# A decoder step on one core: an earlier verdict, later first squares, a second pass without GpSimd, a branch hint, paired last multiplications and stores on two queues

## The chip, the core and the metric

The kernel runs on one core of a Trainium2 chip. The time is device microseconds of one launch. The kernel before took 1876.56 us (median of three runs, 1875.29 to 1877.31).

## The reference

One layer of a hybrid decoder over 264 tokens (256 of a new sequence, 8 single tokens that continue old ones), model width 2048, feed-forward width 5504:

```
h = h + 0.5 * swiglu(rmsnorm(h, norm_ffn1), ffn1_gate, ffn1_up, ffn1_down)
h = h + mixing_block(rmsnorm(h, norm_mix), ...)     # mLSTM heads and a short gated convolution
h = h + 0.5 * swiglu(rmsnorm(h, norm_ffn2), ffn2_gate, ffn2_up, ffn2_down)
y = rmsnorm(h, norm_final)
rmsnorm(x, g) = x * rsqrt(mean(x*x) + EPS) * g
swiglu(x, wg, wu, wd) = (silu(x @ wg) * (x @ wu)) @ wd
```

All inputs and weights are 32-bit floats. The new states of the mixing block are outputs too.

## The kernel before

**Layout.** The width lies on the 128 partitions in KB = 16 blocks, the T = 264 tokens in the free dimension. `h` is 16 tiles of 128x264, two by two in the `hpair` tiles.

**Products.** Each 32-bit weight is split in two 16-bit parts, `whi` (ACT, `high`, L178) and `wlo` (DVE, `low`, L186); each activation likewise, `x[:, 0]` and `x[:, 1]`. `three` (L223) issues three matmuls for one 128x128 block of weights: hi by hi (L224), hi by lo (L225), lo by hi (L226). `fetch` (L192) loads one piece of weights of up to 512 KB through the SP queue and splits it; six buffers each of `wraw`, `whi` and `wlo` let it run ahead. `product` (L228) makes one 128x264 result out of 16 blocks (48 matmuls) and calls `fetch` between its halves.

**The order.** There is no scheduler (`manual_schedule`): each engine runs what the program issues, in that order. `at(n, f)` puts `f` off to a later `tick`; each `product` ticks once at its start and by a half within it.

**The start.** `products4` (L249) makes the first four results (gate and up of two blocks) at once, in nine groups: per group one or two blocks of `h` are loaded, cut in two parts (`Norm.cut`) and squared (`Norm.square`, L372: every second block on ACT, the others on GpSimd, and GpSimd adds them up in `acc`), and a piece of weights serves 24 matmuls (12 in the first two groups). `Norm.finish` (L384) sums `acc` over the partitions with a matmul by ones (`column_sums`, L349) and takes the reciprocal root. It stands right behind `products4` on TensorE.

**The end.** After each of the last 16 products `done` (L459) squares the block on GpSimd and multiplies it by its gain. Behind the last one the root is taken (L329 on ACT, L335 to L341 on DVE), DVE multiplies the 16 blocks by it (L480), and SP stores them (L482, L484).

**The verdict.** 16-bit parts can overflow or lose too much. So `watch` (L288) puts a sum of magnitudes of each result into `stat`, `watch_norm` (L299) two values of each norm's sums into `squares`, and `judge` (L308) tests them against bounds. After the multiplications, the last `judge` calls and matmuls by ones make `bad`, 0 or 1. All five engines load it (L109) and branch on it (L110): if it is 1, the whole step is done again in 32-bit parts, which is a copy of the program of about the same length that stands between the branch and the end. In the usual case all engines jump over it. GpSimd has, behind the jump, an instruction (INC_SWDGE_SEM) that raises the semaphores of its DMA queue as if the copy had run.

Of the kernel before, what the change touches and what calls it, by code (L numbers as in the profile page):

```python
# [8 lines left out]
F32 = mybir.dt.float32  # L9
# [7 lines left out]
SEQ = 256  # L17
# [21 lines left out]
NSTAT = 320  # L39
FIRST = [(0, 1), (1, 1)] + [(k, 2) for k in range(2, KB, 2)]  # L40
# [62 lines left out]
def hymba_step(tc: tile.TileContext, a: dict):  # L103


    with tc.tile_pool(name="verdict", bufs=1) as pool:
        bad = pool.tile([1, 1], mybir.dt.int32, name="bad")
        step(tc, a, bad)
        again = tc.nc.values_load(bad, min_val=0, max_val=1)  # L109
    with tc.If(again > 0):  # L110
        step(tc, a)
# [3 lines left out]
def step(ctx: ExitStack, tc: tile.TileContext, a: dict, bad=None):  # L115
    nc = tc.nc
    PSUM = bass.MemoryType.PSUM
# [4 lines left out]
    AHEAD = 5 if half_size else 2  # L122

# [16 lines left out]
    nc.gpsimd.dma_start(bg, a["bg"])  # L140
# [25 lines left out]
    ident = const.tile([128, 128], F32, name="ident")  # L166
    make_identity(nc, ident)
# [115 lines left out]
    if half_size:  # L283
        stat = const.tile([128, NSTAT], F32, name="stat")
        nc.gpsimd.memset(stat, 2.0 * SUMS[0])
        squares = const.tile([128, 8], F32, name="squares")
# [69 lines left out]
    class Norm:  # L356
# [5 lines left out]
        def block(self, kb, by_act=False):  # L362
            self.cut(kb)
            self.square(kb, by_act)
# [7 lines left out]
        def square(self, kb, by_act=False):  # L372
            new = self.acc is None
            sq = t264("acc", 1) if new else t264("sq")
            if by_act:
                nc.scalar.activation(sq, h[kb], AF.Square)  # L376
            else:
                nc.gpsimd.tensor_tensor(sq, h[kb], h[kb], op=ALU.mult)  # L378
            if new:
                self.acc = sq  # L380
            else:
                nc.gpsimd.tensor_tensor(self.acc, self.acc, sq, op=ALU.add)  # L382

        def finish(self, *rest, last=False):  # L384

            self.r = t264("rstd", 1)
            self.ssum = column_sums(self.acc, *rest)
# [5 lines left out]
    def ffn(layer, norm, done, start=None):  # L393
        with tc.tile_pool(name=f"act_{norm.tag}", bufs=1) as apool:
            first = True
            for half, blocks in enumerate(HALVES):
                act = {}
                for i, j in enumerate(blocks):
                    if start is not None and j < 2:
                        if j == 0:  # L400
                            ps4 = start()
                        pg, pu = ps4[2 * j : 2 * j + 2]
                    else:
                        pg = product((layer, "g", j), norm.x, range(KB))
                        pu = None
# [8 lines left out]
                    if pu is None:  # L414
                        pu = product((layer, "u", j), norm.x, range(KB))
# [19 lines left out]
    def ahead(part):  # L435
# [5 lines left out]
        for kb in range(k0, k0 + n):  # L441
            n1.block(kb, kb % 2 == 0)
# [9 lines left out]
        bank=bank, at=at, tick=tick, watch=watch, high=high, low=low, PART=PART, s3=s3,  # L452
# [6 lines left out]
    def done(kb):  # L459
# [12 lines left out]
    def judge_early():  # L472
        early.append(len(stats))
        judge(stat[:, : early[0]], SUMS)

# [3 lines left out]
    for kb in range(KB):  # L479
        nc.vector.tensor_tensor(h[kb], h[kb], nf.r, op=ALU.mult)  # L480
        if kb < 2:
            nc.sync.dma_start(a["yt"][:, kb, :], h[kb])  # L482
        elif kb % 2:
            nc.sync.dma_start(a["yt"][:, kb - 1 : kb + 1, :], hpair[kb // 2])  # L484

    if half_size:
        watch_norm(nf.ssum)
        judge(stat[:, early[0] : len(stats)], SUMS)
        judge(squares, SQUARES)
        ps = bank()[:1, :1]  # L490
        for i, v in enumerate(verdicts):
            nc.tensor.matmul(
# [593 lines left out]
```

## Time and profile before

| | us |
|---|---|
| three runs, median (range) | 1876.56 (1875.29 to 1877.31) |
| the profiled execution | 1874.37 |
| its span, first to last instruction | 1872.5 |
| time outside the span | 1.87 |
| `products4` on TensorE, first to last matmul | 6.34 to 34.1 |
| last matmul of the last product ends | 1846.9 |
| `bad` is written | 1858.59 |
| last instruction | 1872.5 |

The span counts to the last instruction on any engine, the waiting of sequencers at the end included. Rows of the sequencers (names with a q: SPq, POOLq) are branches, semaphore waits, drains and DMA issues; they are not counted as busy. A time line gives the start and the duration in us, then engine, line, instruction and tiles, and in brackets how long the engine had been idle and what released it.

### The profile page before, as it was taken

Reading aid. Unit: us, or ns where it says so; the run is one execution under the profiler, and the core shown is the slowest. Engines: PE = TensorE matmul, PEld = TensorE weight load, DVE = VectorE, ACT = ScalarE, POOL = GpSimd, SP = SyncE. Lnnn points to the kernel's source line nnn. Section 1 sums busy time; section 2 is a strip of 40 time slices with the busy share of each in tenths; the row PEclk is TensorE's granted clock in tenths of the full one; section 3 lists DMA queues with packets and bytes.
Section 4 is the critical chain, followed back from the end, with each engine's and each line's share of the span. In section 5 each row is a group of like instructions: output and inputs, shape, how many; then the busy total and the mean of one; then the engine's idle time right before and its main releaser. Section 6 shows DMA issues by size and latency. Waiting matters only on the chain.

```text
span 1872.5 us, 38560 instructions
## 1 busy us (share of the span) xinstructions
PE 1830.6 (98%) x16107; PEld 1586.8 (85%) x16107; DVE 1191.9 (64%) x1910; ACT 859.6 (46%) x1211; POOL 146.8 (8%) x219
## 2 busy tenths in 40 slices
PE   8999999999999999999999899999999999999994
PEld 6888888888888888888888688888888888888884
DVE  8666655466666557888888666666655456666453
ACT  6444443344444444656566645444443434444441
POOL 5000000000000211211211021000000000000110
PEclk9999999999999999999999999999999999999997
DMA  7666565656565555878778565656656656655551
GB/s 263 215 198 200 185 206 187 207 189 198 190 199 181 201 187 189 280 236 290 263 236 296 167 206 188 207 188 196 202 189 192 206 187 197 202 188 186 197 192 54
DMA packets 114714, 381.11 MB, mean 204 GB/s; under 512 B 14797, under 2 KB 19997, under 8 KB 114529
## 3 DMA queue, kind: packets, MB, share of 16 engines
q1 hardware_dynamic: 106048, 350.79, 57.4%
q0 software_dynamic: 8192, 27.57, 4.3%
q8 instruction: 128, 2.10, 0.4%
q14 instruction: 58, 0.47, 0.1%
q10 hardware_dynamic: 288, 0.19, 0.1%
HBM read 366.72 MB, written 11.78 MB: 202 GB/s over the span
## 4 chain that ended last, share of the span: by engine, by line
PE 82%; DVE 9%; issue 3%; ACT 2%; DMA 2%; POOL 0%; SPq 0%; DVEq 0%; ACTq 0%; POOLq 0%
PE ps L225 27%; PE ps L224 27%; PE ps L226 27%; DVE wlo L186 3%; DMA rb<-dr 1%; DVE cs L842 1%; ACT whi L178 1%; DVE jk L853 1%; ACT jk L861 1%; ACT L329 0%; DMA wraw<-in_w1gu 0%; DVE x L186 0%; DVE qkv L514 0%; DVE h L480 0%; DVE rs_q L338 0%
## 5 line engine op out<-in xcount | busy, mean ns | idle before, releaser
L186 DVE SCALAR_TENSOR_TENSOR wlo<-wraw,whi 128x1024 f16<-128x1024 f32 (+2 forms) x683 | 787.7, 1194 | 233.7 <-ACT whi L178 233.5
L226 PE MATMUL ps<-x,wlo 128*128 128x264 f16 x2752 | 759.6, 276 | 4.3 <-DVE wlo L186 4.3
L224 PE MATMUL ps<-x,whi 128*128 128x264 f16 x2752 | 759.6, 276 | 1.6 <-ACT whi L178 1.4
L225 PE MATMUL ps<-x,whi 128*128 128x264 f16 x2752 | 759.6, 276 | 0.0
L178 ACT ACTIVATE whi<-wraw 128x1024 f16<-128x1024 f32 (+2 forms) x683 | 664.9, 1016 | 165.5 <-PE ps L225 159.3
L226 PEld LDWEIGHTS <-wlo 128*128 128x128 f16 (+1 forms) x5296 | 518.6, 98 | 84.4 <-DVE wlo L186 6.5
L225 PEld LDWEIGHTS <-whi 128*128 128x128 f16 (+1 forms) x5296 | 518.6, 98 | 81.2 <-issue 1.8
L224 PEld LDWEIGHTS <-whi 128*128 128x128 f16 (+1 forms) x5296 | 518.6, 98 | 80.2 <-ACT whi L178 2.1
L224 PE MATMUL ps<-a,whi 128*128 128x264 f16 x1376 | 379.8, 276 | 0.0
L225 PE MATMUL ps<-a,whi 128*128 128x264 f16 x1376 | 379.8, 276 | 0.0
L226 PE MATMUL ps<-a,wlo 128*128 128x264 f16 x1376 | 379.8, 276 | 0.0
L224 PE MATMUL ps<-xm,whi 128*128 128x264 f16 (+1 forms) x912 | 252.3, 277 | 0.0
L225 PE MATMUL ps<-xm,whi 128*128 128x264 f16 (+1 forms) x912 | 252.3, 277 | 0.0
L226 PE MATMUL ps<-xm,wlo 128*128 128x264 f16 (+1 forms) x912 | 252.2, 276 | 0.0
L178 ACT ACTIVATE a<-tc 128x264 f16<-128x264 f32 x86 | 36.4, 423 | 295.0 <-DVE tc L418 292.6
L413 ACT ACTIVATE tb<-ta 128x264 f32<-128x264 f32 x86 | 36.3, 423 | 224.0 <-DVE ta L410 222.1
L425 DVE SCALAR_TENSOR_TENSOR h<-ps,h 128x264 f32<-128x264 f32 x64 | 27.7, 433 | 159.5 <-PE ps L226 159.5
L417 DVE TENSOR_TENSOR tc<-ps,rstd 128x264 f32<-128x264 f32 x86 | 37.1, 432 | 94.5 <-PE ps L226 94.5
L378 POOL TENSOR_TENSOR acc<-h 128x264 f32<-128x264 f32 x3 | 1.9, 626 | 1177.0 <-DVE stat L294 589.1
L410 DVE TENSOR_TENSOR ta<-ps,rstd 128x264 f32<-128x264 f32 x86 | 37.2, 432 | 60.4 <-PE ps L226 60.2
L186 DVE SCALAR_TENSOR_TENSOR a<-tc,a 128x264 f16<-128x264 f32 x86 | 37.3, 433 | 42.2 <-ACT a L178 42.2
L382 POOL TENSOR_TENSOR acc<-acc,sq 128x264 f32<-128x264 f32 x59 | 55.2, 936 | 6.4 <-ACT sq L376 1.8
(184 smaller groups left out, 864.8 us busy)
## 6 DMA issues: line engine op xcount, KB each, us to landing
wraw<-in_w2gu SPq DMA_DIRECT2D x172, 512.0 KB, 4.9
wraw<-in_w1gu SPq DMA_DIRECT2D x171, 512.0 KB, 4.8
wraw<-in_win SPq DMA_DIRECT2D x112, 512.0 KB, 5.5
wraw<-in_w1d SPq DMA_DIRECT2D x80, 448.0 KB, 4.1
wraw<-in_w2d SPq DMA_DIRECT2D x80, 448.0 KB, 4.0
wraw<-in_wout SPq DMA_DIRECT2D x32, 512.0 KB, 4.5
rb<-dr POOLq DMA_DIRECT2D x16, 513.0 KB, 10.2
wraw<-in_w1d SPq DMA_DIRECT2D x16, 512.0 KB, 4.4
```

Source lines behind the costliest of these rows:

```text
L178: nc.scalar.activation(dst, src, AF.Copy, scale=scale)
L186: nc.vector.scalar_tensor_tensor(dst, src, scale, hi, op0=ALU.mult, op1=ALU.subtract)
L224: nc.tensor.matmul(ps, wh, xk[:, 0, :], start=first, stop=False)
L225: nc.tensor.matmul(ps, wh, xk[:, 1, :], start=False, stop=False)
L226: nc.tensor.matmul(ps, wl, xk[:, 0, :], start=False, stop=last)
L382: nc.gpsimd.tensor_tensor(self.acc, self.acc, sq, op=ALU.add)
L410: nc.vector.tensor_tensor(zg, pg, norm.r, op=ALU.mult)
L413: nc.scalar.activation(sg, zg, AF.Silu)
L417: nc.vector.tensor_tensor(zu, pu, norm.r, op=ALU.mult)
L425: nc.vector.scalar_tensor_tensor(h[db], ps, 0.5 / (sw * sa[layer]), h[db], op0=ALU.mult, op1=ALU.add)
L842: nc.vector.scalar_tensor_tensor(c[:, b, eb], rb[:, b, HD : 2 * HD], self.v[eb][:, col : col + 1], c[:, b, eb], op0=ALU.mult, op1=ALU.add,)
L853: nc.vector.tensor_tensor(jk, c, rb[:, :, :HD].unsqueeze(2).to_broadcast([128, 2, 2, HD]), op=ALU.mult)
```

## The change

**Start.** The first block of `h` is loaded through SP ahead of the first weights, the vectors through ACT alone. `products4` only cuts the blocks. The squares are taken on ACT by pairs of blocks (128x528) behind it, at ticks 0, 1, 1.5 and 2, and GpSimd adds seven pairs into the first. Two products more (gate and up of the third block) come ahead of `norm.finish`, whose sum is made of two matmuls, one for each half of the pair. So the four first results wait in their banks for two products.

**End.** The 16 multiplications become eight of 128x528, and the stores, one for each, go to SP and ACT in turn. The sums of the last norm are tested by an added ACT instruction (L508) that writes into `stat`. The tests of the other norms move to the early `judge`, eight products ahead of the end; the last test is two DVE instructions, of which the second counts, and one more matmul. It stands behind the first multiplication, and `bad` is written behind the second.

**The branch.** Only SP, ACT, TensorE and DVE load `bad` and branch. The second pass uses SP's queue and DVE where the first uses GpSimd (`queue`, `side`), so that no GpSimd instruction is left in it, and takes its mask from `beyond`, which the first pass makes. A bounds check of the loaded value is left out. A hint, "likely taken", stands ahead of the branch on the four engines, behind `bad`.

```diff
+BRANCHING = [getattr(mybir.EngineType, e) for e in ("SP", "Activation", "PE", "DVE")]
...
-    with tc.tile_pool(name="verdict", bufs=1) as pool:
-        step(tc, a, bad)
-        again = tc.nc.values_load(bad, min_val=0, max_val=1)
-    with tc.If(again > 0):
-        step(tc, a)
+        step(tc, a, shared, bad)
+        again = nc.values_load(
+            bad, engines=BRANCHING, min_val=0, max_val=1,
+            skip_runtime_bounds_check_because="a comparison writes 0 or 1",
+        )
+        with tc.If(again > 0, label="again"):
+            step(tc, a, shared)
...
+    queue = nc.gpsimd if half_size else nc.sync
+    side = nc.gpsimd if half_size else nc.vector
...
-    nc.scalar.dma_start(h[0], a["xt"][:, 0, :])
     nc.scalar.dma_start(vecs, a["vecs"])
+    nc.sync.dma_start(h[0], a["xt"][:, 0, :])
...
+        def square_pairs(self, pool, pairs):
+            for i in pairs:
+                tag = f"sq{min(i, 1)}"
+                sq = pool.tile([128, 2, T], F32, tag=tag, name=tag, bufs=1 + 2 * min(i, 1))
+                nc.scalar.activation(sq, hpair[i], AF.Square)
+                if i == 0:
+                    self.acc = sq
+                else:
+                    side.tensor_tensor(self.acc, self.acc, sq, op=ALU.add)
...
+                    if first and start is not None:
+                        ps4 = start()
+                        for n, ps in enumerate(ps4):
+                            early[n // 2, "gu"[n % 2]] = ps
+                        for step, pairs in ((0, (0, 1)), (1, (2, 3)), (1.5, (4, 5)), (2, (6, 7))):
+                            at(step, norm.square_pairs, apool, pairs)
+                        tick(0)
+                        for which in "gu":
+                            early[2, which] = product((layer, which, 2), norm.x, range(KB))
...
-            n1.block(kb, kb % 2 == 0)
+            n1.cut(kb)
...
+                nc.scalar.activation(
+                    t264("ta"), nf.ssum, AF.Copy, scale=2.0**10, accum_out=stat[:, j : j + 1]
+                )
...
+    def scaled(i):
+        r = nf.r.unsqueeze(1).to_broadcast([128, 2, T])
+        nc.vector.tensor_tensor(hpair[i], hpair[i], r, op=ALU.mult)
+        queues[i % 2].dma_start(a["yt"][:, 2 * i : 2 * i + 2, :], hpair[i])
+
+    scaled(0)
     if half_size:
-        watch_norm(nf.ssum)
-        judge(stat[:, early[0] : len(stats)], SUMS)
-        judge(squares, SQUARES)
...
+        counted, least = judge_late()
+        scaled(1)
+        nc.vector.tensor_scalar(bad, counted, least, None, op0=ALU.is_lt)
+
+        tc.no_sync_barrier()
+        tc.mark_branch_hint_location("again", "LikelyTaken", engines=BRANCHING)
+        tc.no_sync_barrier()
+    for i in range(1 + half_size, KB // 2):
+        scaled(i)
```

The order on ACT at the end of `products4` before (`x` a cut block, `sq` its square, `whi` the weights' high part, `rs_y` the first estimate of the root):

```order
L178 ACTIVATE x_423<-h_85,gains 128x264
L376 ACTIVATE sq<-h_85 128x264
L178 ACTIVATE x_429<-h_85,gains 128x264
L178 ACTIVATE whi<-wraw 128x1024 x6
L329 ACT_TABLE_LOAD
L329 ACTIVATE rs_y<-ps,ps_2.384185791015625e-07_115 128x264
L413 ACT_TABLE_LOAD
```

and after, at the same place:

```order
L197 ACTIVATE x_385<-h_87,gains 128x264
L197 ACTIVATE x_388<-h_87,gains 128x264
L197 ACTIVATE whi<-wraw 128x1024 x6
L405 ACTIVATE sq_475<-h_80 128x528
L405 ACTIVATE sq_477<-h_81 128x528
L405 ACTIVATE sq_480<-h_82 128x528
L405 ACTIVATE sq_483<-h_83 128x528
L197 ACTIVATE whi<-wraw 128x1024
L405 ACTIVATE sq_517<-h_84 128x528
L405 ACTIVATE sq_520<-h_85 128x528
L405 ACTIVATE sq_547<-h_86 128x528
L405 ACTIVATE sq_550<-h_87 128x528
```

The square has left the groups; eight squares of pairs stand behind the last six weight pieces of `products4`, with one weight piece among them.

DVE at the end of the program before (`h` the blocks, `ok` and `verdict` the tests):

```order
L480 TENSOR_TENSOR h_85<-h_85,rstd 128x264 x2
L304 TENSOR_REDUCE squares<-ps 128x1 x2
L312 TENSOR_SCALAR ok<-stat 128x9
L313 SCALAR_TENSOR_TENSOR ok<-stat,ok 128x9
L317 TENSOR_REDUCE verdict_23238<-ok 128x1
L312 TENSOR_SCALAR ok<-squares 128x8
L313 SCALAR_TENSOR_TENSOR ok<-squares,ok 128x8
L317 TENSOR_REDUCE verdict_23243<-ok 128x1
L496 TENSOR_SCALAR some<-ps 1x1
L497 CAST bad<-some 1x1
L109 TENSOR_LOAD bad
```

and after, from the root on:

```order
L360 SCALAR_TENSOR_TENSOR rstd<-rs_q,rs_y 128x264
L313 TENSOR_REDUCE stat<-ps 128x1
L545 TENSOR_TENSOR h_80<-h_80,rstd 128x528
L525 TENSOR_SCALAR ok<-stat 128x10
L527 SCALAR_TENSOR_TENSOR ok,count<-stat,ok 128x10
L545 TENSOR_TENSOR h_81<-h_81,rstd 128x528
L552 TENSOR_SCALAR bad<-ps 1x1
L1137 BRANCH_PREFETCH_HINT
L545 TENSOR_TENSOR h_82<-h_82,rstd 128x528
```

The tests have moved from behind the multiplications to between the first two; five more multiplications follow, and then the load of `bad`.

GpSimd at the end of the first pass before (the last row belongs to the second pass):

```order
L378 TENSOR_TENSOR sq<-h_85 128x264
L382 TENSOR_TENSOR acc<-acc,sq 128x264
L109 TENSOR_LOAD bad
L110 COMPARE_AND_BRANCH
L140 DMA bg<-in_bg 64x1
```

and after:

```order
L398 TENSOR_TENSOR acc<-acc,sq 128x264
L394 TENSOR_TENSOR sq<-h_87 128x264
L398 TENSOR_TENSOR acc<-acc,sq 128x264
L121 UNCONDITIONAL_BRANCH
L1137 ISA
```

GpSimd now goes from its last addition straight to the end of the program, whose closing instructions (a drain, a wait for the four other engines, the clearing of the semaphores) it runs there.

More of the change, by code (lines that the diff above doesn't have):

```diff
@@ L360, in __init__, with block @@
             self.tag, self.col, self.x, self.acc = tag, col, [None] * KB, None
-        def block(self, kb, by_act=False):
+        def block(self, kb):
             self.cut(kb)
-            self.square(kb, by_act)
+            self.square(kb)
         def cut(self, kb):
@@ L370, in cut, with square @@
             return x
[L372 removed]
+        def square(self, kb):
             new = self.acc is None
             sq = t264("acc", 1) if new else t264("sq")
[L375 to L378, printed above, removed]
+            side.tensor_tensor(sq, h[kb], h[kb], op=ALU.mult)
             if new:
@@ L381, in square @@
             else:
-                nc.gpsimd.tensor_tensor(self.acc, self.acc, sq, op=ALU.add)
+                side.tensor_tensor(self.acc, self.acc, sq, op=ALU.add)
[7 more added lines that the diff above has]
+                else:
+                    side.tensor_tensor(self.acc, self.acc, sq, op=ALU.add)
         def finish(self, *rest, last=False):
             self.r = t264("rstd", 1)
-            self.ssum = column_sums(self.acc, *rest)
+            acc = [self.acc] if len(self.acc.shape) == 2 else [self.acc[:, i] for i in range(2)]
+            self.ssum = column_sums(*acc, *rest)
             rsqrt(self.r, self.ssum, D, 1.0 if last else 1.0 / (sw * sx))
@@ L394, in ffn, with gate_up @@
         with tc.tile_pool(name=f"act_{norm.tag}", bufs=1) as apool:
+            early = {}
+            def gate_up(j, which):
+                return early.pop((j, which), None) or product((layer, which, j), norm.x, range(KB))
             first = True
@@ L398, in ffn @@
                 for i, j in enumerate(blocks):
[L399 to L405, printed above, removed]
+                    if first and start is not None:
[7 more added lines that the diff above has]
+                            early[2, which] = product((layer, which, 2), norm.x, range(KB))
+                    pg = gate_up(j, "g")
                     if first:
@@ L451, in step @@
         product=product, split=split, rsqrt=rsqrt, column_sums=column_sums, t264=t264,
-        bank=bank, at=at, tick=tick, watch=watch, high=high, low=low, PART=PART, s3=s3,
+        bank=bank, at=at, tick=tick, queue=queue, side=side, half_size=half_size,
+        beyond=beyond, watch=watch, high=high, low=low, PART=PART, s3=s3,
         out_scale=1.0 / (sw * s3),
@@ L474, in judge_early, with judge_late @@
         judge(stat[:, : early[0]], SUMS)
+        judge(squares, SQUARES)
+    def judge_late():
+        late = stat[:, early[0] : len(stats)]
+        n = len(stats) - early[0]
+        ok = tmp.tile([128, 2, n], F32, tag="ok", name="ok", bufs=1)
+        nc.vector.tensor_scalar(ok[:, 0], late, SUMS[0], None, op0=ALU.is_ge)
+        count = const.tile([128, 1], F32, name="count")
+        nc.vector.scalar_tensor_tensor(
+            ok[:, 1], late, SUMS[1], ok[:, 0], op0=ALU.is_le, op1=ALU.mult, accum_out=count
+        )
+        ps = bank()[:1, :1]
+        for i, v in enumerate(verdicts):
+            nc.tensor.matmul(ps, v, ones[:, :1], start=(i == 0), stop=False)
+        nc.tensor.matmul(ps, count, ones[:, :1], start=False, stop=True)
+        return ps, 128.0 * (len(verdicts) + n) - 0.5
     if half_size:
@@ L478, in step @@
     ffn("2", n2, done)
[L479 to L484, printed above, removed]
-    if half_size:
-        watch_norm(nf.ssum)
-        judge(stat[:, early[0] : len(stats)], SUMS)
-        judge(squares, SQUARES)
-        ps = bank()[:1, :1]
-        for i, v in enumerate(verdicts):
-            nc.tensor.matmul(
-                ps, v, ones[:, :1], start=(i == 0), stop=(i == len(verdicts) - 1)
-            )
-        some = const.tile([1, 1], F32, name="some")
-        nc.vector.tensor_scalar(some, ps, 128.0 * len(verdicts) - 0.5, None, op0=ALU.is_lt)
-        nc.vector.tensor_copy(bad, some)
+    queues = (nc.sync, nc.scalar)
+    def scaled(i):
[3 more added lines that the diff above has]
+    scaled(0)
+    if half_size:
+        counted, least = judge_late()
[6 more added lines that the diff above has]
+        scaled(i)
 def mix(tc, a, nm, n2, h, e):
```

91 lines of the change are left out of this document (57 added, 34 removed).

## The prediction

> **What bounds the kernel now.** I read the page first, then the chain of waits, then the time lines of the first 35 us and of the last 30.
>
> ```profile
> span 1872.5 us, 38560 instructions
> PE 1830.6 (98%) x16107; PEld 1586.8 (85%) x16107; DVE 1191.9 (64%) x1910; ACT 859.6 (46%) x1211; POOL 146.8 (8%) x219
> PE 82%; DVE 9%; issue 3%; ACT 2%; DMA 2%; POOL 0%; SPq 0%; DVEq 0%; ACTq 0%; POOLq 0%
> ```
>
> TensorE bounds the middle, which the change leaves alone. What can move is the two ends, where it waits or has finished.
>
> At the start `products4` runs in groups of 24 matmuls. Time lines of TensorE, DVE, GpSimd and ACT, then two pieces of the chain:
>
> ```profile
> 11.30 0.29 PE L226 MATMUL ps<-x,wlo 128*128 128x264 f16 x1 [0.86 <-DVE wlo L186]
> ...
> 14.79 0.28 PE L224 MATMUL ps<-x,whi 128*128 128x264 f16 x1
> ...
> 15.91 0.28 PE L225 MATMUL ps<-x,whi 128*128 128x264 f16 x1
> ```
>
> ```profile
> 14.53 1.86 DVE L186 SCALAR_TENSOR_TENSOR x<-h,gains,x 128x264 f16<-128x264 f32 x2
> 16.31 1.64 DVE L186 SCALAR_TENSOR_TENSOR wlo<-wraw,whi 128x1024 f16<-128x1024 f32 x1
> ```
>
> ```profile
> 16.06 0.81 POOL L378 TENSOR_TENSOR sq<-h 128x264 f32<-128x264 f32 x1
> 16.95 2.50 POOL L382 TENSOR_TENSOR acc<-acc,sq 128x264 f32<-128x264 f32 x2
> ```
>
> ```profile
> 16.13 0.42 ACT L376 ACTIVATE sq<-h 128x264 f32<-128x264 f32 x1 [1.17 <-POOL acc L382]
> ```
>
> ```profile
> 31.42 0.29 PE ps L226
> ...
> 34.07 0.45 PE ps L353 x2
> ```
>
> The first use of a low part comes at 11.30 in the third group and at 31.42 in the ninth: (31.42 - 11.30) / 6 = 3.35 us a group. The ten matmuls from 14.79 to 15.91 took 0.112 each, so a group needs 24 x 0.112 = 2.69. DVE fills the 3.35 (1.86 + 1.64, overlapping), GpSimd too (0.81 + 2.50), and ACT waits for GpSimd. The same instructions elsewhere:
>
> ```profile
> L186 DVE SCALAR_TENSOR_TENSOR xm<-h,gains,xm 128x264 f16<-128x264 f32 x16 | 7.9, 494 | 9.3 <-ACT xm L178 9.3
> L186 DVE SCALAR_TENSOR_TENSOR wlo<-wraw,whi 128x1024 f16<-128x1024 f32 x519 | 617.1, 1227 | 184.3 <-ACT whi L178 184.0 <-issue 0.2
> L178 ACT ACTIVATE x<-h,gains 128x264 f16<-128x264 f32 x32 | 16.3, 508 | 46.3 <-DVE h L993 44.4 <-DVE gains L165 1.7 <-DMA h<-in_xt 0.2
> L178 ACT ACTIVATE whi<-wraw 128x1024 f16<-128x1024 f32 x519 | 519.0, 1042 | 93.5 <-PE ps L225 88.7 <-issue 4.1 <-DMA wraw<-in_w1gu 0.5
> ```
>
> Without GpSimd beside it DVE takes 2 x 0.49 + 1.23 = 2.22 us a group, ACT 2 x 0.51 + 1.04 = 2.06: both below 2.69.
>
> At the end nothing computes for 14 us. Time line of DVE and windows (engine columns, then clock, DMA share, GB/s), then the sequencers' instructions by line (durations min/median/max in ns, first and last start):
>
> ```profile
> 1850.64 5.59 DVE L480 TENSOR_TENSOR h<-h,rstd 128x264 f32<-128x264 f32 x16
> ...
> 1858.45 0.14 DVE L497 CAST bad<-some 1x1 int32<-1x1 f32 x1
> ```
>
> ```profile
> 1856.00:1858.00 2.00, 0.19 (x2) 0.09 (x2) 1.82 (x9) 0.00 (x0) 0.00 (x0) 0.50 0.99 371
> 1858.00:1860.00 2.00, 0.19 (x2) 0.09 (x2) 0.29 (x2) 0.00 (x0) 0.00 (x0) 0.50 0.00 1
> 10.00:20.00 10.00, 8.13 (x68) 6.39 (x69) 9.98 (x10) 7.45 (x15) 9.54 (x9) 1.00 1.09 362
> 1040.00:1042.00 2.00, 0.00 (x0) 0.00 (x0) 1.66 (x5) 0.32 (x1) 0.00 (x0) 0.50 0.84 274
> ```
>
> ```profile
> L109 DVEq TENSOR_LOAD <-bad x1: 545/545/545, 1858.6 to 1858.6; - x1
> ```
>
> ```profile
> L110 SPq EVENT_SEMAPHORE  x8: 17/17/17, 1863.2 to 1863.7; - x8
> ...
> L110 PEldq COMPARE_BRANCH  x1: 3764/3764/3764, 1859.2 to 1859.2; - x1
> ...
> L110 ACTq EVENT_SEMAPHORE  x1: 17/17/17, 1862.9 to 1862.9; - x1
> ...
> L110 DVEq EVENT_SEMAPHORE  x1: 21/21/21, 1863.4 to 1863.4; - x1
> L110 POOLq INC_SWDGE_SEM  x1: 1716/1716/1716, 1863.7 to 1863.7; - x1
> ```
>
> ```profile
> L1066 SPq EVENT_SEMAPHORE  x14: 17/28/28, 1865.3 to 1872.5; - x14
> ...
> L1066 POOLq DRAIN  x3: 46/98/6271, 1865.4 to 1872.2; - x3
> L1066 SPq DRAIN  x3: 7/7/7, 1866.1 to 1871.9; - x3
> ```
>
> The verdict is written at 1858.59; the load takes until 1859.2; the jump costs each engine some 4 us (TensorE shows it in the branch, 3.76, ACT and DVE as nothing until 1862.9 and 1863.4); INC_SWDGE_SEM runs to 1865.4; then a drain of GpSimd of 6.27 ends at 1871.7, while SP had drained at 1866.1. The stores were done by 1858.0. So four things in a row, after the last byte of output: verdict, jump, INC_SWDGE_SEM, drain.
>
> **The change, part by part.**
>
> *Squares out of `products4`.* A square and two additions on GpSimd and a square on ACT leave each group. What is late next is TensorE itself: six groups at 2.69 in place of 3.35 give 6 x 0.66 = -4.0 us. DMA isn't late: a group moves 0.5 MB of weights and 0.26 of `h`, which at 362 GB/s (window 10 to 20) is 2.1 us. The swapped first loads change nothing that lasts, since the third group waits for its data anyway.
>
> *Squares behind it.* Rows for the new pieces:
>
> ```profile
> L869 ACT ACTIVATE sq<-ha 128x528 f32<-128x528 f32 x4 | 2.5, 630 | 0.0
> ```
>
> ```profile
> L382 POOL TENSOR_TENSOR acc<-acc,sq x59: 740/897/1777, 5.9 to 1841.1; 128x264 f32<-128x264 f32 x59
> ```
>
> ```profile
> 30.36 1.61 POOL L382 TENSOR_TENSOR acc<-acc,sq 128x264 f32<-128x264 f32 x1
> ```
>
> The last matmul of `products4` moves to about 34.1 - 4.0 = 30.1; the two products in between cover 2 x 48 x 0.112 = 10.8 us, so the sum is due at 40.9. ACT reaches the squares when its six weight pieces are through, by my estimate at 28.5 (they arrive at 362 GB/s and need free buffers), so the first addition can start at 29.8. An addition of 528 columns isn't in the trace. Below: twice the quiet 0.74, 1.48, seven of them 10.4, ready at 40.2, no wait. Above: twice the 1.61 beside a busy DVE, 3.22, seven 22.5, ready at 52.3, a wait of 11.4. I take it near the lower end, 1.7 each, 41.7, since DVE has only about four low parts of 1.2 to make in these 11 us: a wait of +0.8. The other queues: ACT's squares of pairs 4 to 7 wait for a free one of three buffers, and the weights behind them wait with them; four pieces stand ready, 10.8 us of matmuls, which also cover the elementwise work of three blocks on DVE. The second ones-matmul costs TensorE 0.45 (row at 34.07). Start: -4.0 + 0.8 + 0.45 = **-2.7**.
>
> The Trainium skill, SBUF — State Buffer, "SBUF: two separate sides", calls the port that DVE and GpSimd share an exclusive lock, held for a whole instruction. Taken strictly, it makes additions and low parts alternate: 7 x 1.48 + 4 x 1.23 = 15.3, ready at 45.1, a wait of 4.2 in place of 0.8, and a start of +0.7 (an estimate by the Trainium skill's rule). The trace agrees only in part: DVE's 2.22 quiet and two quiet additions and a square on GpSimd, 2 x 0.74 + 0.81, would not fit in 3.35 if nothing overlapped.
>
> *Multiplications by pairs, stores on two queues.*
>
> ```profile
> L853 DVE TENSOR_TENSOR jk<-cs,rb 128x1024 f32<-128x1024 f32 x16 | 19.5, 1218 | 0.0
> ```
>
> ```profile
> out_yt<-h SPq DMA_DIRECT2D x7, 264.0 KB, 2.2
> ```
>
> 264 columns took 5.59 / 16 = 0.35 from start to start, 1024 1.22 each; between them 528 is about 0.63, eight 5.0. The two tests and `bad` put 0.6 between: the last multiplication ends at 1856.2 as before. The stores are full from 1856 to 1858 (share 0.99), so a second queue gives nothing; the last one, issued at 1856.3, lands 2.2 later, 1858.5. No gain here, 0.5 lost.
>
> *Verdict, jump, GpSimd.* The tests behind the multiplications go: the load on DVE stands at 1856.3 instead of 1858.6. The hint has from 1852.6 on to bring the jump's target, so I take the 3.7 to 4.2 us as hidden; the added ACT instruction runs beside DVE's first multiplication. GpSimd's last addition starts at 1841.1 and nothing holds it from draining behind it: 1842 + 6.3 is long before 1858, and INC_SWDGE_SEM is gone. What is late next is the landing of the last store, 1858.5, for which SP waits behind the jump. Then: SP's remaining waits, 3 in the jump's block and 12 at the end, 0.06 to 0.07 each (1863.2 to 1863.7 for 8; 1865.3 to 1866.1 for 12), 1.0; from there what came before from GpSimd's drain on, 1872.5 - 1871.7 = 0.8, and 0.1 for the barrier. End at 1860.4 instead of 1872.5: **-12.1**.
>
> Sum: -2.7 - 12.1 = -14.8. The profiled execution would come to 1874.37 - 14.8 = 1859.6, its span to 1857.7. It lay 2.2 below the median of the runs, so the median comes to 1876.56 - 14.8 = **1861.8**.
>
> **The rivals.**
>
> *The hint brings nothing* (wrong side of the branch, or fetched too late under full stores). Then ACT, whose last store I take as issued by 1856.7, loads until 1857.2 and stands until 1861.0, DVE until 1856.9 + 4.2 = 1861.1; two waits of SP, 0.2, and 0.9 follow: 1862.2. The landing of the stores hides the rest, so this costs only 1.8: 1863.6. The Trainium skill, Runtime: NRT & Kernel Launch, "Instruction fetch mechanics", speaks for it: prefetch there is purely sequential, and a taken branch to a far target stalls for its fetch. By that the jump stays as long as it is; the trace agrees on the stall (3.76 on TensorE), and shows no hint. 0.22.
>
> *GpSimd's additions become the wait.* With 2.4 each the sum is ready at 46.6, 5.7 late instead of 0.8: +4.9. The clock may halve too, as it did in a gap of TensorE in the mixing block (0.50 in the window 1040 to 1042); at half speed for as long as the gap lasts, +2.9. 1861.8 + 7.8 = 1869.6; with 2.0 each it is 1864, with strict turns of additions and low parts (15.3 for the seven, above) 1865.2. For it: 1.61 in the trace; against it: DVE had six low parts in a row there. 0.13.
>
> *GpSimd still ends last.* Its drain is no leftover of INC_SWDGE_SEM but starts with the others' end: +6.3 from the last wait, 1868. Against it: its queue holds nothing between the last addition and the drain. 0.05.
>
> *Slower: the second pass runs.* The verdict now counts: each of 128 partitions must give ten passes, and the added value, a sum over 264 columns of the norm's sums times 1024, must lie in bounds made for other sums. One miss, and all four engines fall through the branch into the second pass, at least another 1831 us of TensorE: over 3700. It decides at a single count. The sums are near 2048 or more, times 264 x 1024 that is at least 2^29, between 2^20 and 2^60. 0.01.
>
> **How the numbers follow.** Forecast 0.58; the rivals 0.22, 0.13, 0.05 and 0.01; 0.01 for a loss I don't see. Low end: no wait for the sum (-0.8), stores landing 1.8 after issue (-0.4) and a run at the lower edge of the three (-1.3), 1859.3. High end: hint and half of the late additions together, 1861.8 + 1.8 + 4, 1867.6. 0.2% or 3.8 us is about what a measurement can tell here; only the upper bound of the late additions (a wait of 11.4, and the clock with it) comes within it. Faster 0.95, same 0.03, slower 0.02.
>
> **What would show it.** Right: groups of 2.7 us; the first column sum due near 41; GpSimd's drain near 1840 (earlier by the start's gain); branch to next row under 0.5 us; SP released last by a store. Wrong: a gap on TensorE ahead of the first column sum over 2 us; 3 to 4 us behind the branches; GpSimd's drain still the last row.

## The result and the profile after

| | before | after |
|---|---|---|
| median of 5 runs, us | 1876.56 (1875.29 to 1877.31) | 1865.78 (1864.44 to 1866.74) |
| ratio of the times | | 0.9942, 95% interval 0.9928 to 0.9955 |
| profiled execution, us (its span) | 1874.37 (1872.5) | 1866.74 (1865.0) |
| start of the last accumulation of layer 2 | 1846.95 | 1848.90 |
| from there to the end of the span | 25.6 | 16.1 |

The change is 10.8 us faster by the medians; the forecast was 14.8. The profiled execution of before lies 2.2 us under its median, that of after 1.0 over. In this pair all of the gain lies behind the last accumulation: 25.6 - 16.1 = 9.5 us. Ahead of it the changed kernel is 1.95 us late.

The page:

```profile
span 1865.0 us, 38529 instructions
PE 1834.1 (98%) x16109; PEld 1586.7 (85%) x16109; DVE 1184.4 (64%) x1899; ACT 863.0 (46%) x1213; POOL 135.6 (7%) x205
```

TensorE has 3.5 us more of busy time than before, with two matmuls more. That is the first sign of a lower clock (`nohint`, a run below without a lower clock in the start, has 1831.7). The start, windows of the engines (busy time and count of TensorE, its weight loads, DVE, ACT, GpSimd; then clock, DMA share, GB/s):

```profile
20.00:30.00 10.00, 10.00 (x91) 8.68 (x89) 8.63 (x11) 7.72 (x9) 0.00 (x0) 1.00 1.00 382
40.00:42.00 2.00, 1.08 (x10) 0.68 (x7) 2.00 (x2) 1.81 (x2) 1.92 (x2) 1.00 0.01 2
42.00:44.00 2.00, 0.98 (x4) 0.78 (x5) 2.00 (x1) 0.00 (x0) 0.96 (x1) 0.99 0.52 145
44.00:46.00 2.00, 2.00 (x10) 1.32 (x9) 1.18 (x4) 1.70 (x2) 0.00 (x0) 0.50 0.55 197
```

From 20 to 30 us TensorE is full: the groups of `products4` no longer wait for DVE. Then it stands 0.92 + 1.02 = 1.94 us, and 1 us after it goes on, from 44.0, the clock is halved: 10 matmuls start in 2 us where 20 fit. Who was late is told by the time lines of ACT, GpSimd, TensorE and DVE, and by the chain of waits, in this order:

```profile
28.18 1.06 ACT L197 ACTIVATE whi<-wraw 128x1024 f16<-128x1024 f32 x1 [0.21 <-DMA wraw<-in_w1gu]
29.43 1.06 ACT L197 ACTIVATE whi<-wraw 128x1024 f16<-128x1024 f32 x1 [0.19 <-DMA wraw<-in_w1gu]
30.40 2.23 ACT L405 ACTIVATE sq<-h 128x528 f32<-128x528 f32 x4
```

```profile
31.64 11.33 POOL L409 TENSOR_TENSOR sq<-sq,sq 128x528 f32<-128x528 f32 x7 [27.99 <-ACT sq L405]
```

```profile
40.80 0.28 PE L245 MATMUL ps<-x,wlo 128*128 128x264 f16 x1
43.02 1.22 PE L372 MATMUL ps<-sq,ones 128*128 128x264 f32 x4 [1.94 <-POOL sq L409]
```

```profile
39.62 4.43 DVE L205 SCALAR_TENSOR_TENSOR wlo<-wraw,whi 128x1024 f16<-128x1024 f32 x2 [4.20 <-ACT whi L197]
```

```profile
39.42 1.32 POOL sq L409
...
40.81 2.17 POOL sq L409
```

ACT stands behind the weight pieces, each of which waits for its DMA; GpSimd begins at 31.64 and adds for 11.33 us; TensorE has started the last matmul ahead of the column sum at 40.80 and starts the sum at 43.02.

The end. Two pieces of DVE's time line, then the sequencers' rows of the load (L117), the branch (L121) and the closing (L1137), with durations min/median/max in ns, first and last start:

```profile
1848.90 0.43 DVE L461 SCALAR_TENSOR_TENSOR h<-ps,h 128x264 f32<-128x264 f32 x1 [6.57 <-PE ps L245]
```

```profile
1854.14 0.14 DVE L552 TENSOR_SCALAR bad<-ps 1x1 int32<-1x1 f32 x1
1854.20 3.78 DVE L545 TENSOR_TENSOR h<-h,rstd 128x528 f32<-128x528 f32 x6
```

```profile
L117 DVEq TENSOR_LOAD <-bad x1: 602/602/602, 1854.3 to 1854.3; - x1
L117 PEldq TENSOR_LOAD <-bad x1: 590/590/590, 1854.3 to 1854.3; - x1
L117 SPq TENSOR_LOAD <-bad x1: 569/569/569, 1858.3 to 1858.3; - x1
L117 ACTq TENSOR_LOAD <-bad x1: 1077/1077/1077, 1858.8 to 1858.8; - x1
```

```profile
L121 SPq EVENT_SEMAPHORE  x8: 17/17/17, 1862.8 to 1863.4; - x8
...
L121 PEldq COMPARE_BRANCH  x1: 4376/4376/4376, 1855.0 to 1855.0; - x1
...
L121 SPq COMPARE_BRANCH  x1: 70/70/70, 1859.0 to 1859.0; - x1
...
L121 ACTq COMPARE_BRANCH  x1: 68/68/68, 1859.9 to 1859.9; - x1
L121 ACTq EVENT_SEMAPHORE  x1: 17/17/17, 1863.2 to 1863.2; - x1
```

```profile
L1137 POOLq DRAIN  x3: 46/99/7074, 1843.0 to 1864.7; - x3
L1137 SPq DRAIN  x3: 7/7/7, 1864.2 to 1864.5; - x3
```

The verdict is written at 1854.28 and TensorE and DVE load it at once, DVE while its six other multiplications still run (to 1857.98). SyncE and ACT can't: their loads stand behind their own last stores, 1858.3 and 1858.8. Then both jump, 1859.0 to 1862.8 and 1859.9 to 1863.2, as long as before and hint or no hint. SyncE's eight waits behind the jump pass without waiting, so the stores had landed. GpSimd's long drain, 7.07 us, now stands at 1843.0 beside the last products.

### The profile page after: what moved, and what is told of

Same layout as the page of the kernel before. It is cut to its first block, busy times and chain, and to the rows that moved or that the text cites. A ratio compares the mean times of both kernels' runs of the same rounds, so it can differ in the third digit from the quotient of the medians.

```text
span 1865.0 us, 38529 instructions
## 1 busy us (share of the span) xinstructions
PE 1834.1 (98%) x16109; PEld 1586.7 (85%) x16109; DVE 1184.4 (64%) x1899; ACT 863.0 (46%) x1213; POOL 135.6 (7%) x205
## 4 chain that ended last, share of the span: by engine, by line
PE 83%; DVE 7%; issue 3%; ACT 2%; DMA 2%; POOL 1%; SPq 0%; DVEq 0%; ACTq 0%; POOLq 0%
PE ps L243 28%; PE ps L244 28%; PE ps L245 28%; DVE wlo L205 3%; DMA rb<-dr 1%; ACT whi L197 1%; DMA wraw<-in_w1gu 1%; DVE cs L913 1%; POOL sq L409 1%; DVE jk L924 1%; ACT jk L932 0%; PE ps L372 0%; DVE rs_q L357 0%; ACT L348 0%; DVE rs_q L354 0%
## 5 line engine op out<-in xcount | busy, mean ns | idle before, releaser
L313 DVE TENSOR_REDUCE stat<-ps 128x1 f32<-128x16 f32 x310 | 51.3, 165 | 0.0
```

Of the source, the lines that this page charges most:

```text
L313: nc.vector.tensor_reduce(stat[r, j : j + 1], ps[r, T - SEEN : T], axis=mybir.AxisListType.X, op=ALU.add, apply_absolute_value=True,)
```

## The experiments

Two numbers of each profiled kernel keep the ends apart from the middle: the end of the first accumulation of layer 1 (A: what the start did) and the time from the end of the last accumulation of layer 2 to the end of the span (T: the tail). Both are taken from the time line of DVE and the span. Between the two the instructions are the same in all kernels, but for the tests of the other norms, which the change moved there; they took 1589.0 us before, 1589.2 to 1590.5 in twelve of the others and 1591.5 in one. That is why A and T say more than the whole. The clock column says from when on in the start (us) TensorE's clock was at half, for 3.4 us each time.

| kernel | median, us | ratio to before (95%) | A | half clock at | T |
|---|---|---|---|---|---|
| before | 1875.1 to 1876.6 | | 258.4 | none | 25.1 |
| after | 1865.78 | 0.9942 (0.9928 to 0.9955) | 258.9 | 44.0 | 15.7 |
| nohint | 1865.22 | 0.9942 (0.9928 to 0.9955) | 257.8 | none | 15.7 |
| flip | 1865.04 | 0.9947 (0.9933 to 0.9960) | 256.6 | none | 15.6 |
| nobranch | 1861.51 | 0.9921 (0.9907 to 0.9934) | 257.6 | none | 12.3 |
| late | 1864.16 | 0.9941 (0.9928 to 0.9955) | 257.1 | none | 15.4 |
| pool | 1864.90 | 0.9943 (0.9930 to 0.9957) | 259.1 | 44.3 | 15.7 |
| poolwork | 1867.87 | 0.9963 (0.9949 to 0.9977) | 257.9 | 12.6 | 17.6 |
| oneq | 1865.20 | 0.9951 (0.9937 to 0.9964) | 256.8 | none | 15.9 |
| oldload | 1864.92 | 0.9937 (0.9923 to 0.9950) | 258.7 | 43.1 | 15.9 |
| oldstart | 1866.36 | 0.9951 (0.9938 to 0.9965) | 259.2 | 12.1 | 15.7 |
| halfsum | 1864.01 | 0.9935 (0.9922 to 0.9949) | 257.8 | 12.8 | 16.4 |
| earlysq | 1862.79 | 0.9934 (0.9921 to 0.9948) | 255.3 | none | 15.7 |
| best | 1863.20 | 0.9938 (0.9925 to 0.9952) | 255.6 | none | 15.3 |

### The hint and the jump: nohint, flip, nobranch

```diff
-        tc.no_sync_barrier()
-        tc.mark_branch_hint_location("again", "LikelyTaken", engines=BRANCHING)
-        tc.no_sync_barrier()
```

> The changed kernel without the prefetch hint. Theory A (the hint does nothing for this branch): the time stays at the changed kernel's 1865.8 us, within 1 us, and SyncE still shows 3.8 us from its COMPARE_BRANCH to its next row. Theory B (the hint shortens the jump and something else held SyncE up): the row behind the branch comes later still, by up to 1.8 us, and the time rises to some 1867.6 us.

The rows of its branch, as those above:

```profile
L121 SPq EVENT_SEMAPHORE  x8: 17/17/17, 1861.3 to 1861.9; - x8
...
L121 PEldq COMPARE_BRANCH  x1: 3944/3944/3944, 1853.5 to 1853.5; - x1
...
L121 SPq COMPARE_BRANCH  x1: 45/45/45, 1857.1 to 1857.1; - x1
```

SyncE's next row comes 4.2 us behind its branch, TensorE's branch takes 3.94, and T is 15.7 as with the hint. Theory A: the hint does nothing here. Whether it fetched the wrong arm is what `flip` asks:

```diff
-        with tc.If(again > 0, label="again"):
-            step(tc, a, shared)
+        with tc.If(again < 1, label="again", preferred_fallthrough_block=False) as once:
+            pass
+        with once.Else():
+            step(tc, a, shared)
```

> The changed kernel with its condition turned round: the usual case is now the arm of the condition that holds and lies far off, and the general pass is the other arm and stands next; the hint is kept as it is. Theory A (no hint helps here): 1865.8 us, within 1 us, jump of SyncE still 3.8 us. Theory C (the hint in the changed kernel fetched the arm that stands next anyway, because its usual case is the arm of a condition that does not hold): here the jump of SyncE falls under 1 us, its waits begin near 1860 instead of 1862.8, the last stores (their traffic ends at 1861.4) become the end, and the time falls by some 1.8 us to 1864.0 us.

The same rows:

```profile
L121 SPq EVENT_SEMAPHORE  x8: 17/17/17, 1859.5 to 1860.0; - x8
...
L121 SPq COMPARE_BRANCH  x1: 70/70/70, 1855.4 to 1855.4; - x1
```

4.1 us again, T 15.6. Theory C falls: with the usual case as the far arm of a condition that holds, the hint helps no more. A hint that stands earlier, or of another kind, was not tried. What a branch without cost would give:

```diff
-        again = nc.values_load(
...
-        with tc.If(again > 0, label="again"):
-            step(tc, a, shared)
```

> The changed kernel without hint, load and branch; the general pass is left out, so the verdict is written and read by nobody. This is what a branch at no cost would give. If the jump alone ends the program now: the traffic of the last stores ends at 1861.4, twelve waits and the closing exchange take 2.0 us, so 1863.4 against 1865.0 in the profile, 1.7 us less: 1864.1 us. If the stores themselves are held up by the branching (two of them took 1.50 and 0.87 us to issue where the others take 0.34, while VectorE and TensorE were jumping): up to 1.2 us less again, 1862.9 us. If the stores are late by themselves and the jump is hidden: 1865.8 us.

ACT's stores, as issues and with the median time from issue to landing (us, the last number), first in the changed kernel:

```profile
L546 ACTq DMA_DIRECT2D out_yt<-h x4: 338/402/1498, 1854.2 to 1858.3; - x4
```

```profile
out_yt<-h ACTq DMA_DIRECT2D x4, 264.0 KB, 4.6
```

and then in `nobranch`:

```profile
L540 ACTq DMA_DIRECT2D out_yt<-h x4: 338/339/347, 1852.7 to 1856.4; - x4
```

```profile
out_yt<-h ACTq DMA_DIRECT2D x4, 264.0 KB, 2.3
```

T is 12.3, 3.4 us less, more than the 1.7 of the jump alone and the 2.9 with late stores: the jump goes, and the stores are issued without a hitch too (0.35 us at most; in the changed kernel one took 1.50) and land in half the time. So branch and jump cost 3.4 us of the tail, where the rival in the prediction had priced them at 1.8.

### The early verdict and GpSimd: late, pool, poolwork

```diff
-    scaled(0)
-    if half_size:
-        counted, least = judge_late()
-        scaled(1)
-        nc.vector.tensor_scalar(bad, counted, least, None, op0=ALU.is_lt)
...
-    for i in range(1 + half_size, KB // 2):
-        scaled(i)
+    for i in range(KB // 2):
+        scaled(i)
+    if half_size:
+        counted, least = judge_late()
+        nc.vector.tensor_scalar(bad, counted, least, None, op0=ALU.is_lt)
```

> The changed kernel with the verdict behind the eight multiplications and without the hint. Now SyncE's load stands 8.6 to 9.0 us behind the last accumulation, because its own last store is issued at 8.1. Theory V1 (the early verdict is worth only the chain of the verdict behind the last multiplication, about 1.2 us, less what SyncE and ACT wait for their stores anyway): 0.8 us more, 1866.5 us, loads of all engines near 9.8 us behind the last accumulation. Theory V2 (the forecast: 2.3 us): 1868.1 us. Theory V3 (no worth, the stores hold the load as long): 1865.7 us.

DVE's time line, and SyncE's load:

```profile
1849.92 5.04 DVE L545 TENSOR_TENSOR h<-h,rstd 128x528 f32<-128x528 f32 x8
```

```profile
L117 SPq TENSOR_LOAD <-bad x1: 1073/1073/1073, 1855.7 to 1855.7; - x1
```

The load stands 9.05 us behind the end of the last accumulation on all engines. In the changed kernel TensorE and DVE have it at 5.0, but SyncE at 9.0 and ACT at 9.5. T is 15.4 against 15.7: V3, the place of the verdict is worth nothing here. What ends last is not the same: here no engine jumps before the last store is issued, the stores land in 2.3 to 2.4 us, SyncE's jump takes 2.7 us (1856.9 to 1859.6), and TensorE's jump, from 1857.0 to 1861.0, is the last. An early verdict lets TensorE and DVE jump sooner, and the stores that are then under way land later. The verdict's length brought the load forward: from the end of the last multiplication to the load it was 1856.23 to 1858.6 before and is 1854.96 to 1855.7 here, 1.6 us shorter, since there are no reductions over 264 columns at the end and one pair of tests instead of two. What that alone is worth in T was not run.

For GpSimd, first only in load, hint and branch (`"DVE", "Pool"` in `BRANCHING`), then with its work in the general pass as well:

```diff
-BRANCHING = [getattr(mybir.EngineType, e) for e in ("SP", "Activation", "PE", "DVE")]
+BRANCHING = [getattr(mybir.EngineType, e) for e in ("SP", "Activation", "PE", "DVE", "Pool")]
...
-    queue = nc.gpsimd if half_size else nc.sync
-    side = nc.gpsimd if half_size else nc.vector
+    queue = nc.gpsimd
+    side = nc.gpsimd
```

> The changed kernel with GpSimd as a fifth engine of load, hint and branch; the general pass still gives it no work. Theory P1 (the long closing drain comes behind any branch that GpSimd takes part in): drain of 6.3 us or more behind GpSimd's jump, near 10 to 17 us behind the last accumulation, the end at 18 to 19 us instead of 15.6, so about 3 us more: 1868.7 us. Theory P2 (drain and INC_SWDGE_SEM come only with a general pass that works on GpSimd): no change, 1865.7 us.

GpSimd's branch in `pool`, and its closing drains:

```profile
L121 POOLq COMPARE_BRANCH  x1: 70/70/70, 1854.9 to 1854.9; - x1
```

```profile
L1137 POOLq DRAIN  x3: 46/104/6271, 1855.1 to 1864.7; - x3
```

GpSimd drains for 6.27 us behind its branch, but from 1855.1: without anything to jump over it needs 0.2 us behind the branch, and there is no INC_SWDGE_SEM. It ends at 1861.4, before SyncE's jump does (1862.7). T 15.7, no change; P1's drain came, its place was wrong.

> The changed kernel with GpSimd's work given back to the general pass and GpSimd back in load, hint and branch. Theory P1 (with work of its own in the arm that is jumped, GpSimd jumps 3.3 to 4 us, then does INC_SWDGE_SEM, 1.7 us, and drains, 6.3 us): load at 5.0 us behind the last accumulation, jump done near 9.5, INC_SWDGE_SEM to 11.3, drain to 17.6, end near 18.5 instead of 15.6: 2.9 us more, 1868.3 us. Theory P2 (the early verdict hides all of it): 1865.4 us. Had GpSimd's rows cost only what the forecast gave them, 6.3 us with nothing ahead of them hidden, it would be 1872 us.

The rows of the branch in `poolwork`, and its closing drains:

```profile
L121 POOLq EVENT_SEMAPHORE  x5: 17/43/43, 1855.4 to 1855.8; - x5
L121 POOLq COMPARE_BRANCH  x1: 68/68/68, 1852.8 to 1852.8; - x1
...
L121 POOLq INC_SWDGE_SEM  x1: 1716/1716/1716, 1855.8 to 1855.8; - x1
```

```profile
L1137 POOLq DRAIN  x3: 46/104/6269, 1857.6 to 1864.4; - x3
L1137 SPq DRAIN  x3: 7/7/7, 1862.0 to 1864.1; - x3
```

Jump 2.6 us, five waits, INC_SWDGE_SEM 1.72 and drain 6.27 in a row from 1852.8 to 1863.9, while SyncE had drained at 1862.0. T is 17.6, 1.9 more, and the median is the highest of all changed kernels: P1, smaller since GpSimd's jump was shorter than taken. Set beside `late` this says how the tail's gain is made up. With GpSimd in the branch and an early verdict T is 17.6, from 25.1. With GpSimd out and a late verdict it is 15.4. With GpSimd out and an early one, 15.7. Either edit does most of the work, though both steps from 25.1 hold the shorter verdict as well, and GpSimd in the branch with a short late verdict was not run. Beside the early verdict taking GpSimd out adds 1.9; beside GpSimd's leaving the early verdict adds nothing.

### Stores and loads: oneq, oldload

```diff
-    queues = (nc.sync, nc.scalar)
+    queues = (nc.sync, nc.sync)
```

> The changed kernel with all eight stores on SyncE's queue, pairs kept. Theory Q1 (what ends the program is SyncE's jump behind its last store, and the queues matter only through when that store is issued): last store issued near 8.7 us behind the last accumulation instead of 8.1 to 9.0, load near 9.0, jump done near 13.2 to 13.8, time 1865.8 us within 0.5. Theory Q2 (the second queue shortens the transfers): traffic of the stores ends some us later, past the jump, 1867 us or more. Theory Q3 (ACT's jump and stores delay SyncE's): SyncE's jump shortens from 3.9 to 4.2 us towards 2.7, time 1864.8 us.

SyncE's stores and its branch:

```profile
L546 SPq DMA_DIRECT2D out_yt<-h x8: 332/360/1334, 1850.4 to 1855.8; - x8
```

```profile
L121 SPq EVENT_SEMAPHORE  x8: 17/17/17, 1859.6 to 1860.7; - x8
...
L121 SPq COMPARE_BRANCH  x1: 70/70/70, 1857.1 to 1857.1; - x1
```

T 15.9, 0.2 more: the time is Q1's. One issue took 1.33 us, so the last store was late and the load stood at 9.9 instead of 9.0; the jump behind it was 2.5 instead of 3.8, which was Q3's sign, and the eight waits behind the jump took 1.1 us instead of 0.6. SyncE's jump is as short in `late` and `best` (2.7 and 2.9) and 3.8 to 4.9 in the nine other changed kernels with a branch; why is not shown.

```diff
-    nc.scalar.dma_start(vecs, a["vecs"])
-    nc.sync.dma_start(h[0], a["xt"][:, 0, :])
+    nc.scalar.dma_start(h[0], a["xt"][:, 0, :])
+    nc.scalar.dma_start(vecs, a["vecs"])
```

> The changed kernel with the first two loads as before: the first block of h ahead of vecs, both on ACT's queue. With the changed loads and no lower clock in the first 60 us, the first accumulation of the first layer ended at 257.2 us (mean of five profiled kernels, 256.6 to 257.8), against 258.4 before. Theory L1 (most of those 1.2 us come from the loads, whose first product in DVE stood 1.1 us earlier): first accumulation back near 258.2 us, 1866.5 us. Theory L2 (the forecast: the loads change nothing that lasts): first accumulation at 257.2 us (258.9 if the lower clock falls into the start), 1865.4 us.

A is 258.7 with a half clock from 43.1 on, behind the wait; without those 1.7 us it would be 257.0, where L1 had 258.2. L2: as far as one execution tells, the first loads change nothing that lasts.

### The start: oldstart, halfsum, earlysq

The squares back in `products4` by ACT and GpSimd in turn, the sum right behind it, no products ahead:

```diff
         for kb in range(k0, k0 + n):
             n1.cut(kb)
+            if half_size:
+                n1.square_early(kb)
```

> The changed kernel with the start of before: squares by ACT and GpSimd in turn inside products4, first column sum right behind it, no products put ahead. It prices the start. Theory S1 (the start is worth what the three runs without a lower clock there show, 0.6 to 1.8 us at the end of the first layer's first half): the time rises by about 1.1 us, to 1866.9 us, and the last accumulation of the second layer stands about 1 us later. Theory S2 (the forecast's own sum, 2.7 us): 1868.5 us. Theory S3 (the start is worth nothing or costs, as the profiled run of the changed kernel has it, plus 0.5 us): 1865.3 us. Trace, all theories: TensorE idle about 2 us again between 20 and 38 us, no wait of TensorE near 41 us.

The engines' windows (TensorE, its weight loads, DVE, ACT, GpSimd; clock, DMA share, GB/s):

```profile
20.00:30.00 10.00, 8.93 (x78) 7.07 (x76) 10.00 (x10) 7.39 (x13) 9.53 (x10) 1.00 0.72 254
30.00:38.00 8.00, 7.52 (x66) 6.22 (x64) 8.00 (x7) 6.63 (x7) 2.68 (x3) 1.00 0.68 209
```

DVE full, TensorE idle for 1.55 us of these 18, no wait later: the mechanism is back. The size isn't settled. A is 259.2 with a half clock from 12.1 on. Had it cost its full 1.7 us, A would be 257.5 without it, 0.3 later than the 257.2 of the five kernels that have the changed start and no half clock. But DVE is the limit there: TensorE's idle time up to 38 us is 6.0 where it was 7.0 before, so the half clock is partly hidden. The kernel before, with the same squares and no half clock, has 258.4, 1.2 later. The median's ratio, 0.9951, lies 0.0009 above the changed kernel's, 1.7 us, with intervals that overlap. The new start is worth between 0.3 and 1.7 us.

```diff
+                        if half_size:
+                            at(1.5, norm.finish)
+                            early[3, "g"] = product((layer, "g", 3), norm.x, range(KB))
+                            first = False
```

> The changed kernel with the first column sum put off by half a product: the third gate product is put ahead and the sum stands in its middle, 2.7 us later for TensorE. Theory G (TensorE's wait of 1.9 us for GpSimd's last additions, near 41 to 43 us, is what the start lost, and the lower clock of the 3.4 us behind it follows from that wait): both go, 1.9 and 1.7 us, and the time falls to some 1862.2 us. Theory H (the lower clock comes whatever TensorE waits): 1.9 us less, 1863.9 us. Theory J (the wait only moves, to TensorE's fourth up product, which needs a bank that the first gate block frees behind the root): no change, 1865.8 us.

The same windows in `halfsum`:

```profile
12.00:14.00 2.00, 1.48 (x8) 1.07 (x9) 1.91 (x4) 1.74 (x4) 0.00 (x0) 0.69 1.07 375
14.00:16.00 2.00, 2.00 (x11) 1.32 (x9) 1.87 (x4) 1.71 (x4) 0.00 (x0) 0.50 1.08 368
40.00:42.00 2.00, 2.00 (x21) 1.74 (x19) 1.57 (x1) 2.00 (x3) 1.84 (x3) 1.00 0.02 8
42.00:44.00 2.00, 2.00 (x20) 1.75 (x18) 2.00 (x2) 0.54 (x2) 1.80 (x1) 1.00 0.13 49
```

The wait is gone and the clock stays at 1.00 there; J falls. In the profiled execution, the slowest of its five, the half clock came earlier instead, behind a wait for the first weights, so A shows 257.8; SyncE's jump took 4.9 us in it, and T is 16.4. The median, 1864.01, is H's (by the ratios 1.3 us below the changed kernel's, with intervals that overlap); how often the lower clock falls into the start, one profile can't tell.

The squares of the first four pairs issued inside `products4`:

```diff
         for kb in range(k0, k0 + n):
             n1.cut(kb)
+        if half_size and k0 in (12, 14):
+            n1.square_pairs(pools[0], (k0 - 12, k0 - 11))
...
-                        for step, pairs in ((0, (0, 1)), (1, (2, 3)), (1.5, (4, 5)), (2, (6, 7))):
+                        for step, pairs in ((0, (4, 5)), (1, (6, 7))):
```

> The changed kernel with the squares of its first four pairs issued inside products4, ahead of the last weight pieces, the other four behind it. Theory G (TensorE's 1.7 to 2.3 us of waiting near 41 to 43 us come from ACT's late squares and GpSimd's seven additions in a row behind them): the last addition is ready near 38 us, the wait goes, and the time falls by some 1.9 us, to 1863.9 us, without another halfway sum. Theory K (additions beside VectorE's wlo slow the groups of products4, where TensorE then waits again): the period of the groups rises over 2.7 us, and the gain is used up: 1865.8 us.

GpSimd's time line, and the windows:

```profile
23.91 2.79 POOL L409 TENSOR_TENSOR sq<-sq,sq 128x528 f32<-128x528 f32 x2 [1.85 <-ACT sq L405]
31.59 8.63 POOL L409 TENSOR_TENSOR sq<-sq,sq 128x528 f32<-128x528 f32 x4 [4.89 <-ACT sq L405]
```

```profile
20.00:30.00 10.00, 9.87 (x89) 8.35 (x87) 8.40 (x10) 8.73 (x13) 4.02 (x3) 1.00 0.87 327
...
40.00:42.00 2.00, 2.00 (x16) 1.66 (x14) 1.30 (x1) 0.00 (x0) 0.21 (x1) 1.00 0.80 287
```

G: the last addition ends at 40.2 (38 was expected; the four together took 8.63), just in time. TensorE loses 0.13 us from 20 to 30 and nothing behind it. A is 255.3, 1.9 below the 257.2 of the five. K, the additions beside `wlo`, costs next to nothing.

### Both: best

`earlysq` and `late` in one kernel, without the hint.

> The changed kernel with both findings so far: the squares of the first four pairs inside products4, and the verdict behind the multiplications, without the hint. If the two add up: the start 1.9 us earlier and the tail 0.3 us shorter (15.3 us behind the last accumulation), 1862.5 us against 1864.9 to 1865.8 for the changed kernel and 1875.5 to 1876.6 before. If the tail's 0.3 us was chance: 1862.8 us.

A 255.6 and T 15.3: both parts are there. Its median, 1863.20, and `earlysq`'s, 1862.79, are the lowest of the kernels that keep the general pass, 2.6 and 3.0 us under the changed kernel's; by the ratios to before it is 0.8 and 1.5 us. The intervals overlap with the changed kernel's, so that they are faster rests on A, which is read in one execution each.

## Why the prediction was right and where it was not

The time came 4.0 us above the forecast and inside the range. The course that the forecast gave 0.58 did not come: the rival with 0.22 did, and, of the one with 0.13, the late sum and the half clock without the longer additions. The range held because its high end adds these two up, and because the tail without its jump is 0.8 us shorter than forecast. Of the prediction's own signs of being wrong, 3 to 4 us behind the branches came. By its steps:

- **Groups at 2.69 us, -4.0.** Right in kind. TensorE's idle time up to 38 us was 7.0 before (the windows) and 3.3 after; the eight other kernels with the same groups gave 3.1 to 4.0. The last matmul ahead of the sum starts at 40.80, where the sum was forecast to be due at 40.9.
- **A wait of +0.8 for the sum.** Under-sized: 1.94 in the changed kernel, 1.4 to 2.5 in seven of those eight. The failing step is "ACT reaches the squares when its six weight pieces are through, by my estimate at 28.5". The last ones came 1.25 us apart and each held ACT for its DMA; the squares began at 30.40 and the additions at 31.64, where 29.8 had been taken. The price of an addition was about right: 11.33 / 7 = 1.62, forecast 1.7. `earlysq`, which starts the additions earlier, removes the wait, although they take 2.16 each at its end.
- **The clock.** The forecast had it under a rival with longer additions. In four of nine profiled kernels with this start it fell to half for 3.4 us: three times from 0.4 to 1.1 us after the wait had ended, 1.7 us lost each, and once from 12.6 us on (`poolwork`), where less was lost, since TensorE came later to the sum and waited 0.64 for it. Waits of the same length, 1.89 in `late` and 2.31 in `nohint`, left the clock at 1.00. The five without it had A 1.2 us below before, all nine together 0.6, where the forecast had 2.7. A doubled ones-matmul cost 0.7, not 0.45: two took 0.45 before, four 1.16 in `nohint`. With these the start's sum would be -4.0 + 1.9 + 0.7 = -1.4, near the 1.2.
- **Pairs and two queues, no gain.** Right: 0.63 was taken for a multiplication of 528, the row says 3.78 / 6; a single queue changes T by 0.2. But "the last one, issued at 1856.3, lands 2.2 later" does not hold with the early verdict: the stores' median was 4.6, and 3.9 to 4.9 in all ten kernels that branch with stores still to issue.
- **"the load on DVE stands at 1856.3 instead of 1858.6".** DVE loads even earlier, 5.0 us behind the last accumulation where the forecast had 8.9, and it is beside the point. The step overlooked whose load ends last: SyncE and ACT hold it behind their own stores. `late` gives the same tail.
- **"I take the 3.7 to 4.2 us as hidden".** Wrong, and the largest part of the miss. The first rival was the right mechanism, and under-priced at 1.8; `nobranch` gives 3.4. Counted from the end of the last accumulation, its program ends at 14.8 (1862.2) where the changed kernel's ends at 15.7: it put two of SyncE's waits and 0.9 behind the jumps of ACT and DVE, 1.1 us, while SyncE itself jumps until 1862.8 and 2.2 us follow. The end without a jump, which the price is set against, was taken at 13.0 (1860.4) and is 12.3 in `nobranch`. The Trainium skill, Runtime: NRT & Kernel Launch, "Instruction fetch mechanics", which has prefetch purely sequential and a far taken branch stall, was the better guide: 2.5 to 4.9 us from the branch to the next row on every engine with an arm to jump over, with and without the hint.
- **GpSimd's drain.** Right: at 1843.0, hidden. `poolwork` prices GpSimd's leaving at 1.9 us beside the early verdict.
- **Slower, by a second pass.** It didn't run: the program ends behind one.

Summed: the tail gave -9.5 in place of -12.1 (the jump, +3.4, set against 0.8 more than forecast elsewhere: `nobranch` has -12.9, from 25.14 to 12.27), the start -0.6 to -1.2 in place of -2.7. That is -10.1 to -10.7, and the medians say -10.8. The stretch between the ends is not in this sum: the changed kernels took 0.2 to 2.5 us longer for it than the one profiled execution of before, which lay 2.2 under its median.

The Trainium skill's lock on the port that DVE and GpSimd share (SBUF — State Buffer, "SBUF: two separate sides") would have made the start +0.7. The trace agrees with turns nearly: the addition at 39.42 is not slowed (1.32) by the `wlo` that starts beside it at 39.62, but that `wlo` and the next take 4.43 where two alone take 2.46, and the addition between them takes 2.17. Turns without any overlap would end that addition at 40.74 + 1.23 + 1.31 = 43.28; it ended at 42.98. The estimate was too high mainly by its count: two low parts came between the additions and not four.

## What to carry to other kernels

When a step behind the work is moved forward, ask on which engine it ends last and what that engine still has to issue: an early verdict helps only engines with nothing queued ahead of the load, and here the stores under way landed later beside the jumps. Two edits that each take the same stall off the end don't add up; price each with the other in place. A jump over a long arm cost 2.5 to 4.9 us on each engine whatever was hinted, so it is cheap on engines whose queue runs ahead and dear on the one that issues the last store.

## What the runs showed of the hardware

- The prefetch hint changed nothing in either arrangement of the arms: SyncE's next row came 3.8 us behind the branch with it, 4.2 without, 4.1 with the arms turned round.
- Stores issued while other engines jump can take long: 1.50 us in the changed kernel, 1.33 in `oneq`, and 0.36 at most in `nobranch`, `late` and `best`, where no engine jumps before the last issue. Their median landing was 3.9 to 4.9 us in the ten kernels that jump earlier and 2.2 to 2.4 in these three. What in the jumps is in the way was not tried.
- GpSimd's closing drain takes 6.3 to 7.1 us wherever it stands. INC_SWDGE_SEM, 1.72 us, came only where the skipped arm holds work of GpSimd.
- A half clock lasted 3.4 us in the starts, with the same instructions in some executions and not in others. Why it fell in four of nine is open.
